# Cache attention with score products over 256 keys, turned five channel slices at a time

## The chip, the core and the metric

The kernel runs on one core of a Trainium2 chip. The metric is the device time of one execution in microseconds (us). Of the core's engines, TensorE (PE in the profile; PEld is its weight load) does the matrix products, VectorE (DVE), ScalarE (ACT) and GpSimd (POOL) the rest, and POOL also issues the gathers of this text. SyncE (SP) issues most other transfers. Each engine runs its instructions in the order in which the built program lists them, and waits on semaphores for the others.

## The reference, cut to what matters

The program is one inference step of a two-layer decoder: layer 0 mixes tokens with an mLSTM, layer 1 with multi-head latent attention, and each layer ends in a SwiGLU feed-forward part. It serves one prompt of 1024 new tokens and 8 samples with one new token each. The change lies in layer 1, in the attention of the samples over their caches:

```
# per sample: 8192 past tokens in 64 pages of 128, 8 heads
c_all  = concat(cache_latent[pages], c_new)      # (8193, 256)
kr_all = concat(cache_k_rope[pages], kr_new)     # (8193, 64)
s = (q_lat @ c_all.T + q_rope @ kr_all.T) * SCALE   # (8, 8193)
o = softmax(s) @ c_all                              # (8, 256)
```

The caches are float32. A sample's cached keys are 8192 rows of 256 latent and 64 rotary channels, 10.5 MB, and all 8 samples read 84 MB.

## The kernel before

Layer 1's attention stage runs two things side by side. The prompt's attention is cut into 32 slots (8 heads, 4 blocks of 256 queries; `prompt`, L1700): scores (L1725 to L1732), softmax (L1733 to L1749), transposes of the weights on PE (L1765), their split into a high and a low part (`split_g`, whose low part is L130 on POOL, or `split`, L117 and L118), and the product with the values (L1785). Between the slots `sample_units` (L1850) is advanced, a Python generator. It makes 16 units: each of the 8 samples has two, of 4096 cached keys. `NONE` and `DBL` say after which slots it is advanced not at all, or twice.

A unit in the kernel before is worked in two halves of 2048 keys (`u`):

- Gathers on POOL's queue: two of latent rows into `nat` (L1877, 1 MB each) and two of rotary rows into `nrp` (L1878, 256 KB each). `nat` has four buffers of [128, 16, 256] floats, two units' worth; a buffer comes free when the value products of the unit two before have read it. `nrp` has two.
- Five transposes on DVE (L1885), each of 1024 elements per partition, turn two slices of 32 channels of the half into a `tt` tile (four buffers). I call one **T**.
- Score products on PE (L1892) into `psS`, half of the PSUM tile `ss`: the stationary operand is `qbd`, 128 x 32, and the moving one 128 x 128, a block of turned keys; the four values of `j` write four groups of 32 PSUM partitions. They come in two bursts for a half, one of three `tt` tiles (24 products) and one of two (16). I call such a burst **M**. A float32 product is two records in the trace, so 48 and 32 there.

After both halves the unit's softmax runs (L1897 to L1913): row maximum on DVE, exponential on ACT, one transpose and 16 small copies into `pz`. The value products (L1921, `values()`), **V**, multiply `pz` (128 x 32) with `nat` (256 columns), 32 products or 64 records. They are recorded as `self.due` and written only at the start of the next unit, or inside the next prompt slot. The second unit of a sample is followed by a short epilogue (L1925 to L1943).

What sets the order: the code is not run in the order written. A scheduler in the tile framework places each instruction by its dependences and its own estimate of times; `high_priority(offset=SOON)` lets M and V move ahead of other work, and `issue_after(self.qk)` keeps V behind a prompt product. So a change inside a unit moves the instructions around it on every engine of the stage. Outside the stage the two programs list the same instructions in the same order.

Of the kernel before, what the change touches and what calls it, by code (L numbers as in the profile page):

```python
# [18 lines left out]
P = 128  # L19
# [72 lines left out]
class Kern:  # L92
# [15 lines left out]
    def t(self, pool, shape, tag, dt=F32, bufs=None):  # L108
        self.n += 1
        return pool.tile(shape, dt, tag=tag, name=f"{tag}{self.n}", **({"bufs": bufs} if bufs else {}))  # L110
# [1739 lines left out]
    def sample_units(self, b, first):  # L1850
        nc = self.nc
        V = nc.vector
        pr = self.pr
        t = lambda shape, tag, bufs: self.t(pr, shape, tag, bufs=bufs)
        lat = self.cache_latent.rearrange("l n (r s) c -> (l n r) (s c)", s=8)
        rop = self.cache_k_rope.rearrange("l n (r s) c -> (l n r) (s c)", s=8)
# [8 lines left out]
            self.nb = self.nb0[:, b:b + 1]  # L1865
        ss = self.mmt("ss")
        psS, psV = ss[:, 0:256], ss[:, 256:512]
        keys = []
        for u in range(2):
            nat = t([P, 16, 256], "nat", 4)  # L1870
            nrp = t([P, 16, 64], "nrp", 2)
            keys.append(nat)
            for g in range(2):
                n = b * 8 + (0 if first else 4) + u * 2 + g
                ix = bass.IndirectOffsetOnAxis(ap=self.idx[:, n:n + 1], axis=0)
                s = slice(g * 8, g * 8 + 8)
                nc.gpsimd.indirect_dma_start(out=nat[:, s].rearrange("p s c -> p (s c)"), out_offset=None, in_=lat, in_offset=ix)  # L1877
                nc.gpsimd.indirect_dma_start(out=nrp[:, s].rearrange("p s c -> p (s c)"), out_offset=None, in_=rop, in_offset=ix)  # L1878

            for cps in ((4, 0, 1), (2, 3)):  # L1880
                parts = []
                for cp in cps:
                    tt = t([P, 2, 16, 32], "tt", 4)
                    src = nat[:, :, 64 * cp:64 * cp + 64] if cp < 4 else nrp
                    V.transpose(out=tt, in_=src.rearrange("p s (c i) -> p c s i", i=32))  # L1885
                    parts.append((cp, tt))
                with self.tc.high_priority(offset=SOON):
                    for cp, tt in parts[-1:] + parts[:-1]:
                        for c in range(2):
                            cb = 2 * cp + c  # L1890
                            for j in range(4):
                                nc.tensor.matmul(psS[32 * j:32 * j + 32, u * P:u * P + P], self.qbd[:, b, cb],  # L1892
                                                 tt[:, c, 4 * j:4 * j + 4].rearrange("p s k -> p (s k)"), start=cb == 2, stop=cb == 5)
            if u == 0:
                yield
        rm = t([P, 1], "rm", 2)
        V.reduce_max(rm, psS, axis=AX.X)  # L1897
# [11 lines left out]
        pz = self.pz  # L1909
# [6 lines left out]
        def values():  # L1916
            self.due = None
            with self.tc.high_priority(offset=SOON), self.tc.issue_after(self.qk):
                for i in range(8):
                    for j in range(4):  # L1920
                        nc.tensor.matmul(psV[32 * j:32 * j + 32], pz[:, j, i], keys[i // 4][:, j * 4 + i % 4], start=i == 0, stop=i == 7)  # L1921
            V.scalar_tensor_tensor(acc, acc, al, psV, op0=ALU.mult, op1=ALU.add)
            if not first:
                m = t([P, 1], "m", 1)
                V.tensor_scalar(m, nb, -1.0, None, op0=ALU.mult)  # L1925
                nc.tensor.transpose(ss[0:1, 0:P], m, self.ident)
                mn = t([1, 8], "mn", 1)
                V.reduce_max(mn, ss[0:1, 0:P].rearrange("o (x h) -> o h x", h=8), axis=AX.X)
                mc = t([P, 256], "sS", 1)[0:1, :P].rearrange("o (x h) -> o x h", h=8)
                V.tensor_copy(mc, mn.unsqueeze(1).to_broadcast([1, 16, 8]))  # L1930
                nc.tensor.matmul(ss[:, P:P + 1], mc.rearrange("o x h -> o (x h)"), self.ones[0:1, 0:1], start=True, stop=True)
                fac = t([P, 1], "fac", 2)
                V.tensor_tensor(fac, m, ss[:, P:P + 1], op=ALU.subtract)
                nc.scalar.activation(fac, fac, AF.Exp)
                V.tensor_scalar(lrow, lrow, fac, None, op0=ALU.mult)
                nc.tensor.matmul(ss[:, 256:257], self.ct[:, C_SL:C_SL + P], lrow, start=True, stop=True)
                rl = t([P, 1], "rl", 2)
                V.reciprocal(rl, ss[:, 256:257])
                w = t([P, 8], "w0", 2)
                V.tensor_scalar(w, self.ct[:, C_SL:C_SL + 8], rl, fac, op0=ALU.mult, op1=ALU.mult)  # L1940
                for f in range(2):
                    nc.tensor.matmul(ss[:, 384 + f * 8:392 + f * 8], acc[:, f * P:(f + 1) * P], w, start=True, stop=True)
                V.tensor_copy(self.olat[:, :, :, b], ss[:, 384:400].rearrange("p (f h) -> p f h", f=2))  # L1943
# [166 lines left out]
```

## Time and profile before

| | |
|---|---|
| median of 3 runs | 2581.78 us (2577.17 to 2588.86) |
| the profiled execution | 2603.12 us, span of its instructions 2601.3 us |
| PE, PEld, DVE busy | 2510.5, 2367.6, 1864.6 us |
| ACT, POOL busy | 1328.5, 606.3 us |
| M: records, busy | 2560, 101.7 us |
| V: records, busy | 1024, 62.3 us |
| T: instructions, busy | 160, 192.4 us |
| gathers | 128 (64 `nat`, 64 `nrp`), by issue on POOL 60.8 and 61.5 us |

A row of a group reads: line, engine, operation, out<-in by the program's tile names, shape, xcount | busy us, mean ns of one | idle time of the engine just before them, and what ended most of it. Busy time is a union: products in flight at once count once. A row of the timeline reads: start in us from the span's start, length, engine, line, operation, tiles, shape, xcount; equal neighbours are merged, so a burst is one row, and its end is when its last result is out. The time to the next row's start is the better measure of what it holds PE for.

### The profile page before, as it was taken

How to read it: one execution, taken by the hardware profiler on the slowest of the kernel's cores; microseconds unless marked ns; L12 is line 12 of the kernel's file. 1: busy time of each engine (PE TensorE's matmuls, PEld its weight loads, DVE VectorE, ACT ScalarE, POOL GpSimd, SP SyncE). 2: the span in 40 equal slices, each digit the busy share in tenths (PEclk: the TensorE clock that was granted, in tenths of full speed). 3: DMA queues.
4: the chain of work that ended last, by engine and by line, in shares of the span. 5: the costliest groups of instructions: out<-in, count | busy, mean ns of one | idle time of the engine just before them, and what ended most of it. 6: DMA issues, size and time to landing. Idle time of an engine off the chain costs nothing.

```text
span 2601.3 us, 54299 instructions
## 1 busy us (share of the span) xinstructions
PE 2510.5 (97%) x21151; PEld 2367.6 (91%) x21151; DVE 1864.6 (72%) x4491; ACT 1328.5 (51%) x3282; POOL 606.3 (23%) x636
## 2 busy tenths in 40 slices
PE   8999999999999999999988889999999999999998
PEld 8999987999999999999976767767899999999998
DVE  4345678897777777666557877768498877777765
ACT  4122344465666666554354555656256656556543
POOL 1021222201111111122335545442211111111102
PEclk9999999999999999999988999999999999999999
DMA  6153554427666566654566676664535566665663
GB/s 196 41 83 95 147 138 106 157 78 149 121 129 124 115 122 128 122 163 150 192 226 247 237 259 225 210 242 147 191 106 113 119 129 127 130 127 115 122 137 113
DMA packets 332087, 382.35 MB, mean 147 GB/s; under 512 B 23433, under 2 KB 263054, under 8 KB 323510
## 3 DMA queue, kind: packets, MB, share of 16 engines
q0 software_dynamic: 60992, 186.65, 31.9%
q1 hardware_dynamic: 258838, 182.04, 23.3%
q10 hardware_dynamic: 12000, 10.20, 1.2%
q8 instruction: 166, 2.72, 0.4%
q14 instruction: 91, 0.75, 0.1%
HBM read 253.37 MB, written 125.44 MB: 146 GB/s over the span
## 4 chain that ended last, share of the span: by engine, by line
PE 69%; DVE 9%; DMA 4%; issue 4%; ACT 2%; POOL 1%; SPq 0%; another core or an unknown queue 0%; POOLq 0%; ACTq 0%; DVEq 0%
PE sc L136 12%; PE sc L134 12%; PE sc L135 12%; PE mm L136 5%; PE mm L135 5%; PE mm L134 5%; PE ss L1892 2%; PE ss L134 2%; PE ss L135 2%; PE ss L136 2%; DMA nat<-in_cache_latent_dram,idx 2%; PE ss L1921 2%; DVE tt L1885 2%; PE mm L1785 1%; DVE wl L118 1%
## 5 line engine op out<-in xcount | busy, mean ns | idle before, releaser
L1215 POOL DMA_DIRECT2D x_d<-wl x72 | 86.8, 1206 | 992.6 <-DVE wl L1214 357.1
L117 ACT ACTIVATE wh<-wr 128x512 fp32r<-128x512 f32 (+2 forms) x167 | 133.4, 799 | 199.7 <-PE mm L135 136.1
L1885 DVE STREAM_TRANSPOSE tt<-nat 128x1024 f32<-128x1024 f32 x128 | 155.4, 1228 | 28.6 <-DMA nat<-in_cache_latent_dram,idx 20.4
L1892 PE MATMUL ss<-tt,qbd 128*32 128x128 f32 x2560 | 101.7, 289 | 18.2 <-issue 8.3
L1892 PEld LDWEIGHTS ss<-tt,qbd 128*32 128x32 f32 x2560 | 76.9, 115 | 40.7 <-issue 17.7
L118 DVE TENSOR_TENSOR wl<-wr,wh 128x1024 fp32r<-128x1024 f32 (+2 forms) x80 | 92.8, 1161 | 28.2 <-ACT wh L117 27.0
L117 ACT ACTIVATE b<-u 128x256 fp32r<-128x256 f32 (+1 forms) x252 | 98.5, 414 | 20.4 <-PE ss L136 6.3
L118 DVE TENSOR_TENSOR b<-u,b 128x256 fp32r<-128x256 f32 (+1 forms) x252 | 103.1, 422 | 6.8 <-ACT b L117 5.4
L1215 POOL DMA_DIRECT2D x_d<-st x72 | 102.4, 1422 | 8.6 <-DVE dC L118 3.5
L134 PE MATMUL mm<-zh,wh 128*128 128x344 f32 x320 | 103.5, 323 | 0.0
L135 PE MATMUL mm<-zl,wh 128*128 128x344 f32 x320 | 103.4, 323 | 0.0
L136 PE MATMUL mm<-zh,wl 128*128 128x344 f32 x320 | 103.3, 323 | 0.0
L118 DVE TENSOR_TENSOR wh<-S,wh 128x512 fp32r<-128x512 f32 x108 | 74.5, 690 | 34.6 <-ACT wh L117 34.3
L117 ACT ACTIVATE wh<-S 128x512 fp32r<-128x512 f32 x108 | 67.9, 629 | 44.4 <-PE sc L136 32.1
L1742 ACT ACTIVATE wr<-sc,mx,rqt 128x512 f32<-128x512 f32 (+2 forms) x96 | 64.6, 676 | 39.5 <-DVE mx L1737 22.8
L134 PE MATMUL sc<-zh,wh 128*128 128x344 f32 x256 | 82.9, 325 | 0.2 <-DVE q L432 0.2
L1785 PE MATMUL mm<-wh,vt 128*128 128x256 f32 (+1 forms) x320 | 74.6, 298 | 8.5 <-ACT wh L117 6.3
L135 PE MATMUL sc<-zl,wh 128*128 128x344 f32 x256 | 82.1, 321 | 0.0
L136 PE MATMUL sc<-zh,wl 128*128 128x344 f32 x256 | 82.0, 320 | 0.0
L1878 POOL DMA_INDIRECT nrp<-in_cache_k_rope_dram,idx x64 | 61.5, 961 | 64.5 <-DVE tt L1885 30.2
L905 POOL TENSOR_TENSOR ss<-ss,sq 128x512 f32<-128x512 f32 (+2 forms) x36 | 51.2, 1423 | 99.4 <-ACT sq L904 99.3
L130 POOL TENSOR_TENSOR wl<-spl,wh 128x512 fp32r<-128x512 f32 x43 | 54.7, 1284 | 83.4 <-ACT spl L129 80.8
(1084 smaller groups left out, 10701.6 us busy)
## 6 DMA issues: line engine op xcount, KB each, us to landing
wr<-in_ffn_w_gate_up_dram SPq DMA_DIRECT2D x96, 512.0 KB
x_d<-st POOLq DMA_DIRECT2D x72, 520.0 KB
x_d<-wl POOLq DMA_DIRECT2D x72, 512.0 KB
dr<-in_ffn_w_down_dram SPq DMA_DIRECT2D x72, 256.0 KB
wr<-in_mlstm_w_in_dram SPq DMA_DIRECT2D x24, 512.0 KB
wr<-in_mlstm_w_out_dram SPq DMA_DIRECT2D x16, 512.0 KB
q<-qn_d SPq DMA_DIRECT2D x28, 256.0 KB
wr<-in_mla_w_o_dram SPq DMA_DIRECT2D x14, 512.0 KB
```

Of the source, the lines that this page charges most:

```text
L117: ins = nc.scalar.activation(hi, src, AF.Copy)
L118: self.low = e.tensor_tensor(lo, src, hi.bitcast(F32), op=ALU.subtract)
L130: nc.gpsimd.tensor_tensor(lo, x, hi.bitcast(F32), op=ALU.subtract)
L134: mm(ps, wh, xh, start=start, stop=False, **kw)
L135: mm(ps, wh, xl, start=False, stop=False, **kw)
L136: self.last = mm(ps, wl, xh, start=False, stop=stop, **kw)
L1215: nc.gpsimd.dma_start(self.x_d[:, 2 * dp:2 * dp + 2, 512 * i:512 * i + 2 * PW[i]], st[i], accum_op=ALU.add)
L1742: nc.scalar.activation(px[:, ks], o, AF.Exp, bias=mx[:, 0:1], scale=f, accum_out=sm[:, c:c + 1])
L1785: nc.tensor.matmul(o, x, y, start=i == 0, stop=i == len(ops) - 1)
L1878: nc.gpsimd.indirect_dma_start(out=nrp[:, s].rearrange("p s c -> p (s c)"), out_offset=None, in_=rop, in_offset=ix)
L1885: V.transpose(out=tt, in_=src.rearrange("p s (c i) -> p c s i", i=32))
L1892: nc.tensor.matmul(psS[32 * j:32 * j + 32, u * P:u * P + P], self.qbd[:, b, cb], tt[:, c, 4 * j:4 * j + 4].rearrange("p s k -> p (s k)"), ...
```

## The change

A unit is no longer worked by halves of keys, but by channels. All eight gathers of a unit are issued first, each rotary one before the latent one, into a `nat` of both halves (two buffers, the same bytes) and an `nrp` of both (one buffer, the same bytes). A T turns one slice of 32 channels of both halves. A product moves 256 columns, 128 keys of each half, so a unit has 40 of them (80 records) in place of 80 (160 records). Step 0 turns and multiplies channel slices 0, 8, 9 and then 1, 2 (8 and 9 are the rotary ones); step 1 turns 3, 4, 5 and then 6, 7. There are four bursts in a unit as before, of 12 and 8 products.

```diff
-        keys = []
+        nat = t([P, 2, 16, 256], "nat", 2)
+        nrp = t([P, 2, 16, 64], "nrp", 1)
         for u in range(2):
-            nat = t([P, 16, 256], "nat", 4)
-            nrp = t([P, 16, 64], "nrp", 2)
-            keys.append(nat)
             for g in range(2):
...
-                nc.gpsimd.indirect_dma_start(out=nat[:, s].rearrange("p s c -> p (s c)"), out_offset=None, in_=lat, in_offset=ix)
-                nc.gpsimd.indirect_dma_start(out=nrp[:, s].rearrange("p s c -> p (s c)"), out_offset=None, in_=rop, in_offset=ix)
-
-            for cps in ((4, 0, 1), (2, 3)):
+                nc.gpsimd.indirect_dma_start(out=nrp[:, u, s].rearrange("p s c -> p (s c)"), out_offset=None, in_=rop, in_offset=ix)
+                nc.gpsimd.indirect_dma_start(out=nat[:, u, s].rearrange("p s c -> p (s c)"), out_offset=None, in_=lat, in_offset=ix)
+
+        for step in range(2):
+            for cbs in ((0, 8, 9), (1, 2)) if step == 0 else ((3, 4, 5), (6, 7)):
                 parts = []
-                for cp in cps:
+                for cb in cbs:
                     tt = t([P, 2, 16, 32], "tt", 4)
-                    src = nat[:, :, 64 * cp:64 * cp + 64] if cp < 4 else nrp
-                    V.transpose(out=tt, in_=src.rearrange("p s (c i) -> p c s i", i=32))
-                    parts.append((cp, tt))
+                    src = nat[:, :, :, 32 * cb:32 * cb + 32] if cb < 8 else nrp[:, :, :, 32 * cb - 256:32 * cb - 224]
+                    V.transpose(out=tt.rearrange("p u s k -> p (u s) k"), in_=src.rearrange("p u s c -> p (u s) c"))
+                    parts.append((cb, tt))
                 with self.tc.high_priority(offset=SOON):
-                    for cp, tt in parts[-1:] + parts[:-1]:
-                        for c in range(2):
-                            cb = 2 * cp + c
-                            for j in range(4):
-                                nc.tensor.matmul(psS[32 * j:32 * j + 32, u * P:u * P + P], self.qbd[:, b, cb],
-                                                 tt[:, c, 4 * j:4 * j + 4].rearrange("p s k -> p (s k)"), start=cb == 2, stop=cb == 5)
-            if u == 0:
+                    for cb, tt in parts[-1:] + parts[:-1]:
+                        for j in range(4):
+                            nc.tensor.matmul(psS[32 * j:32 * j + 32], self.qbd[:, b, cb],
+                                             tt[:, :, 4 * j:4 * j + 4].rearrange("p u s k -> p u (s k)"), start=cb == 9, stop=cb == 6)
+            if step == 0:
                 yield
...
-                        nc.tensor.matmul(psV[32 * j:32 * j + 32], pz[:, j, i], keys[i // 4][:, j * 4 + i % 4], start=i == 0, stop=i == 7)
+                        nc.tensor.matmul(psV[32 * j:32 * j + 32], pz[:, j, i], nat[:, i // 4, j * 4 + i % 4], start=i == 0, stop=i == 7)
```

In the program after, M is L1889, V is L1918, T is L1884, and the gathers are L1875 (`nrp`) and L1876 (`nat`). The scheduler's order moves with it. Two places show how; the number behind a tile's name tells the allocations apart.

PE, around the value products of the thirteenth unit (`ss_20857`). Before, the first bursts of the fourteenth unit (`ss_21205`) stand ahead of them, and those of its second half behind:

```order
L1892 MATMUL ss_21205<-tt_21244,qbd_16070 32x128 x8
L1892 MATMUL ss_21205<-tt_21242,qbd_16070 32x128 x8
...
L1732 MATMUL sc_21102<-mk_15334 128x128
L1921 MATMUL ss_20857<-nat_20858,pz_15338 32x256 x16
L1921 MATMUL ss_20857<-nat_20994,pz_15338 32x256 x16
L1892 MATMUL ss_21205<-tt_21379,qbd_16070 32x128 x8
L1892 MATMUL ss_21205<-tt_21375,qbd_16070 32x128 x8
L1892 MATMUL ss_21205<-tt_21377,qbd_16070 32x128 x8
```

After, the same two units are `ss_20353` and `ss_20659`:

```order
L1732 MATMUL sc_20556<-mk_15334 128x128
L1918 MATMUL ss_20353<-nat_20354,pz_15338 32x256 x32
L1889 MATMUL ss_20659<-tt_20674,qbd_16070 32x256 x4
L1889 MATMUL ss_20659<-tt_20670,qbd_16070 32x256 x4
L1889 MATMUL ss_20659<-tt_20672,qbd_16070 32x256 x4
L1785 MATMUL mm_20464<-wh_20454,vt_20013 128x256
```

The first burst of a unit has moved from ahead of the value products of the unit before it to behind them, and each row of products is half as many of twice the width.

POOL, the gathers of the tenth unit and the splits of the prompt (L130) near them. Before, the rotary gathers of the tenth (`nrp_19615`, `nrp_19778`) and eleventh unit are issued early, and the tenth unit's latent ones (`nat_19614`) behind several splits:

```order
L1878 DMA nrp_19615<-in_cache_k_rope_dram,idx_14527 128x512 x2
L1878 DMA nrp_19778<-in_cache_k_rope_dram,idx_14527 128x512 x2
L130 TENSOR_TENSOR kt_18510<-spl_18640,kt_18510 128x512
L130 TENSOR_TENSOR kt_18510<-spl_18651,kt_18510 128x512
L1878 DMA nrp_20043<-in_cache_k_rope_dram,idx_14527 128x512 x2
L130 TENSOR_TENSOR wl_18832<-spl_18838,wh_18831 128x512
L130 TENSOR_TENSOR wl_18832<-spl_18847,wh_18831 128x512
L130 TENSOR_TENSOR vt_18883<-spl_18897,vt_18883 128x512
L130 TENSOR_TENSOR wl_18996<-spl_19002,wh_18995 128x512
L1877 DMA nat_19614<-in_cache_latent_dram,idx_14527 128x2048 x2
```

After, the ninth unit's eight gathers (`nrp_18931`, `nat_18930`) stand together ahead of the splits around them:

```order
L130 TENSOR_TENSOR wl_18319<-spl_18325,wh_18318 128x512
L1875 DMA nrp_18931<-in_cache_k_rope_dram,idx_14527 128x512 x4
L1876 DMA nat_18930<-in_cache_latent_dram,idx_14527 128x2048 x4
L130 TENSOR_TENSOR kt_18242<-spl_18372,kt_18242 128x512
L130 TENSOR_TENSOR kt_18242<-spl_18383,kt_18242 128x512
L130 TENSOR_TENSOR wl_18538<-spl_18544,wh_18537 128x512
L130 TENSOR_TENSOR wl_18538<-spl_18553,wh_18537 128x512
```

A unit's gathers have moved closer to each other, and splits of the prompt now stand behind four latent gathers in a row.

## The prediction

> **What bounds the kernel now.** I read the page first, then the stage in which the units run, by windows, groups, waits, the chain, and the timeline of single bursts.
>
> ```profile
> span 2601.3 us, 54299 instructions
> PE 2510.5 (97%) x21151; PEld 2367.6 (91%) x21151; DVE 1864.6 (72%) x4491; ACT 1328.5 (51%) x3282; POOL 606.3 (23%) x636
> L1892 PE MATMUL ss<-tt,qbd x2560: 269/273/423, 1355.6 to 1779.0; 128*32 128x128 f32 x197
> 1350.00:1790.00 440.00, 394.31 (x5021) 308.38 (x5020) 329.90 (x715) 238.36 (x630) 210.08 (x206) 0.96 0.67 231
> by line: PE ss L1892 14.5%; DMA nat<-in_cache_latent_dram,idx 11.6%; issue 10.0%; PE ss L1921 9.8%; DVE tt L1885 9.2%; PE mm L1785 7.7%; PE mm L1765 2.7%; POOL wl L130 2.5%; DVE pz L1913 2.3%; POOL nrp L1878 2.0%; PE sc L1725 1.9%; PE sc L1
> ```
>
> The third line bounds the stage: M starts at 1355.6 and 1779.0, so I take 1350 to 1790, 440 us of 2601. In this window (PE, PEld, DVE, ACT, POOL busy; PE clock; DMA share; GB/s) PE is busy 394 of 440 us, DVE 330, the DMA engines 0.67. Over the page PE has 97%, here 90%. The last line is the chain in this window: a quarter of it runs through M and the latent gathers' flight, a further fifth through T and V. So PE is nearly full but does not bound the stage alone; the units' own circle (V frees a buffer, gather, T, M, softmax, V) is often what ends last. Nothing outside this stage is touched, so the forecast is a sum over it.
>
> The groups of this window and the waits in it (us in total, times, longest):
>
> ```profile
> L1885 DVE STREAM_TRANSPOSE tt<-nat 128x1024 f32<-128x1024 f32 x128 | 155.4, 1228 | 28.6 <-DMA nat<-in_cache_latent_dram,idx 20.4 <-PE ss L1892 4.2 <-remote 3.5
> L1892 PE MATMUL ss<-tt,qbd 128*32 128x128 f32 x2560 | 101.7, 289 | 18.2 <-issue 8.3 <-DVE tt L1885 7.3 <-DVE sm L1745 1.7
> L1892 PEld LDWEIGHTS ss<-tt,qbd 128*32 128x32 f32 x2560 | 76.9, 115 | 40.7 <-issue 17.7 <-DVE tt L1885 15.0 <-DVE sm L1745 3.5
> L1921 PE MATMUL ss<-nat,pz 128*32 128x256 f32 x1024 | 62.3, 381 | 1.3 <-ACT pz L1913 0.9 <-issue 0.4
> PE ss L1892 <- DVE tt L1885: 7.3, 9, 3.0
> POOL nat L1877 <- PE ss L1921: 14.2, 7, 5.6
> POOL nrp L1878 <- DVE tt L1885: 30.2, 9, 8.2
> POOL wl L130 <- ACT spl L129: 80.8, 18, 17.0
> PE mm L1785 <- ACT wh L117: 5.8, 7, 2.1
> PE mm L1785 <- POOL wl L130: 0.5, 2, 0.3
> ```
>
> The reader is to see that M waits 18.2 us in all (PE idle ahead of it), V 1.3, that T waits 20.4 us for latent gathers, that those wait for V (14.2) and the rotary ones for T (30.2), and that PE hardly ever waits for POOL's split (0.5).
>
> **The change part by part. The products.** 1280 products of 128 columns (2560 records) become 640 of 256 (1280 records). What is a product worth? The group's mean of 289 ns says nothing, since four column groups overlap. The timeline of PE shows bursts without a wait in them:
>
> ```profile
> 1427.56 0.40 PE L1728 MATMUL sc<-kk,qrr 128*128 128x512 f32 x1
> 1427.79 0.39 PE L1730 MATMUL sc<-kl,qrr 128*128 128x512 f32 x1
> ...
> 1593.18 0.28 PE L134 MATMUL mm<-swh,ckh 128*128 128x256 f32 x1
> 1593.30 0.27 PE L135 MATMUL mm<-swl,ckh 128*128 128x256 f32 x1
> 1593.71 1.52 PE L1892 MATMUL ss<-tt,qbd 128*32 128x128 f32 x48
> 1595.16 0.39 PE L136 MATMUL mm<-swh,ckl 128*128 128x256 f32 x1
> ...
> 1596.06 1.08 PE L1892 MATMUL ss<-tt,qbd 128*32 128x128 f32 x32
> 1597.07 0.39 PE L136 MATMUL mm<-swh,ckl 128*128 128x256 f32 x1
> ...
> 1598.84 3.75 PE L1921 MATMUL ss<-nat,pz 128*32 128x256 f32 x64
> 1602.33 1.68 PE L1892 MATMUL ss<-tt,qbd 128*32 128x128 f32 x38
> ```
>
> From start to the next start, 48 records hold PE for 1.45 us and 32 for 1.01. The 16 between them, four groups of four, cost 0.44: 0.110 us for a group of 128 columns, and 1.01 - 8 x 0.110 = 0.13 us is left for the burst, whatever its length. V has the very shape that M gets (32 stationary columns, 256 moving, float32): 64 records, 16 groups, 3.49 us, so 0.218 for a group of 256. Two narrow groups, 0.220, become one wide, 0.218. There are 320 such pairs, so the change saves 0.6 us of PE in 2600. The 0.13 of a burst stays, as there are still four bursts in a unit. If I divide each burst by its records instead, 0.0302 for M (1.45 / 48) and 0.0545 for V, the unit would go from 4.92 to 80 x 0.0545 = 4.36 us, 9.0 us in all; that counts the burst's own 0.13 as the records', and V followed directly by M doesn't pay it. So 0.6, with 0 and 9.0 as ends.
>
> The Trainium skill's page "TensorEngine Tiling (Array Packing)", section Instruction Overhead, gives each matmul about 60 cycles beside its columns, which at the 2.4 GHz of its page "TensorE: Matmul & The Clock Gate" would be, as an estimate, 1280 x 25 ns = 32 us saved. That second page of the Trainium skill, section Back-to-back issue gap, has N / 2.4 + 2.5 ns from one to the next instead, which gives an estimate of 320 x 2.5 ns = 0.8 us. The trace agrees with the second and not with the first: 0.110 and 0.218 us for twice 128 and twice 256 columns.
>
> Two edits go with it. 1280 weight loads fall away; they lie beside the products (76.9 us in PEld, and the 0.110 of a group already holds whatever of them shows): 0. Entering and leaving the narrow form costs PE the 0.13; counted over PE's order the changes between 32 and 128 stationary columns go from 142 to 138, since V and M follow each other more often: -0.3, between 0 and -0.5.
>
> **The transposes.** 160 of 1024 elements before and after, with the same runs of 32 floats: 0 by the row (1228 ns). Nothing covers more than that: at 30 ns more or less each, DVE would have 5 us more or less in 440, of which it is busy 330.
>
> **The gathers and the waits.** This is where the time can move. The same 128 gathers, 0.95 us of POOL each, carry the same bytes. But the first T of a unit (slice 0) now needs all four latent gathers, where it needed two. The price of a pair, from V to T, in the rows of PE, POOL and DVE:
>
> ```profile
> 1456.05 4.01 PE L1921 MATMUL ss<-nat,pz 128*32 128x256 f32 x64
> 1459.69 0.96 POOL L1877 DMA_INDIRECT nat<-in_cache_latent_dram,idx  x1 [0.16 <-issue]
> 1460.96 0.94 POOL L1877 DMA_INDIRECT nat<-in_cache_latent_dram,idx  x1 [0.30 <-issue]
> 1469.03 1.25 DVE L1885 STREAM_TRANSPOSE tt<-nat 128x1024 f32<-128x1024 f32 x1 [3.22 <-DMA nat<-in_cache_latent_dram,idx]
> q0 software_dynamic: 14185, 81.56, 52.4%
> ```
>
> From the first issue to T it is 9.3 us for 2.1 MB. The last row (packets, MB, share of 16 engines in the 440 us) gives the gathers' full rate, 81.56 MB / (0.524 x 440 us) = 354 GB/s: 5.9 us of data, 3.4 around it. Four latent gathers, 4.2 MB, then take 11.8 + 3.4 = 15.2 us, and 18.2 if the 1.05 MB of the rotary ones falls among them. So the first T comes 6 to 9 us later after V than before.
>
> Against it stands more cover. In PE's order I summed the rows between the end of a unit's V and the first M of the unit two later (the one that gets its buffer), each at its pace: 0.110 and 0.218 for groups as above, 0.12 for a 256-wide product (1593.18 to 1593.30), 0.23 for a 512-wide (1427.56 to 1427.79). Over the 14 units it is 9.7 us before (5.3 to 13.2), 18.5 after (15.4 to 22.2): the first M has gone behind the V of the unit ahead of it, as the two pieces of PE's order show. The whole stage sums to 308 us at that pace and takes 440, a stretch of 1.43, so the cover is about 14 us before and 26 after. Needed: before 9.3 + two T, 11.8; after 15.2 to 18.2 + three T, 18.9 to 21.9. The margin of a unit rises from 2 us to between 4 and 7. So I expect fewer waits of T on gathers, and of M on T: a third of M's 18.2, -6, between -18.2 (all of it) and +28 (the slower rival).
>
> What pays for it is the way from a unit's last M to its V, in which the softmax runs: 14.9 us at the same pace before, 7.5 after, and 3.2 to 4.5 in the first five units, 4.6 to 6.4 stretched. The chain's rows have such a way nearly bare:
>
> ```profile
> 1396.44 0.81 PE ss L1892 x18
> ...
> 1402.59 0.40 issue
> 1402.99 4.02 PE ss L1921 x60
> ```
>
> 5.7 us from M's end (1397.25) to V, of which V waited the last 0.40. So V will wait up to a microsecond in the first five units, +3 (0 to 6). And the first unit starts later, since nothing is turned until its fourth latent gather, which now stands behind two splits into `kt`. Its rows in POOL and DVE now:
>
> ```profile
> 1351.70 0.94 POOL L1877 DMA_INDIRECT nat<-in_cache_latent_dram,idx  x1 [0.30 <-issue]
> 1352.65 2.54 POOL L130 TENSOR_TENSOR kt<-spl,kt 128x512 fp32r<-128x512 f32 x2
> 1352.00 1.25 DVE L1885 STREAM_TRANSPOSE tt<-nrp 128x1024 f32<-128x1024 f32 x1 [2.36 <-DMA nrp<-in_cache_k_rope_dram,idx]
> ```
>
> With the splits first, the gather goes out near 1354 and lands some 8 us later (1460.96 to 1469.03 above), 10 us after the 1352.0 at which T begins now. But all ten T of that unit can then follow without a break, and the scheduler has put the first M behind 5 us more of the prompt's products: +1 (0 to 7).
>
> **The sum:** -0.6 - 0.3 - 6 + 3 + 1 = -3 us. The profiled execution took 2603.12 us (1.8 more than its span), 21 above the median of the runs; on it that is 2600, on the median, 2581.8, it is 2579. A measurement of this kernel tells a change of about 0.5%, 13 us, from none.
>
> **The rivals.** *Waits go too (faster).* If the margin is as large as I work out, M may stop waiting at all: -18.2 for M, less the 3 for V and 1 for the start, gives 2567, more if the prompt's products wait less as well. For it speaks the margin; against it that a third of M's idle time is put down to DVE's order and not to gathers, as the transposes of a unit still take 10 x 1.23 us of an engine that has 330 of 440 us of work.
>
> *Cost by the instruction (faster).* If a wide group cost what a narrow one does, M would lose 320 x 0.110 = 35 us: 2547. V's 0.218 speaks against it; only a difference between V's weights or addresses and M's could save it. The first rule of the Trainium skill above ("TensorEngine Tiling (Array Packing)", Instruction Overhead) is on this side.
>
> *The gathers bind (slower).* Each unit's gathers are now one block on POOL, four in a row behind one V, and the prompt's splits (L130) behind them, as the pieces of POOL's order show; a rotary gather of the next unit can't go until T has turned this unit's, which is behind the latent gathers now. If the block's last gather lands over 22 us after V instead of 15 to 18, the cover of 26 us is used up by it and three T. Each microsecond beyond holds M, and with it PE, in 14 units: at 2 us, +28, 2610. The up to 5.6 us that a latent gather waited for V and up to 8.2 of a rotary one on T speak for it, the 0.5 us that PE waited for splits against. The clock is a part of it: over 1400 to 1500 PE was granted 0.95 of it.
>
> ```profile
> 1400.00:1500.00 100.00, 90.42 (x1206) 71.34 (x1205) 78.01 (x168) 50.92 (x140) 52.40 (x52) 0.95 0.69 236
> ```
>
> The Trainium skill's page "TensorE: Matmul & The Clock Gate", section What's actually happening, halves the clock after an idle window of about 3.4 us; one such window in each of the 14 units would by that, as an estimate, cost 14 x 1.7 = 24 us more. The longest wait of M for T in the rows above is 3.0 us, so no run here shows that step yet.
>
> **How the numbers follow.** No change that can be told 0.46 (2579); waits go too 0.28; cost by the instruction 0.03; the gathers bind 0.23. So faster 0.31, same 0.46, slower 0.23. The range reaches past the first faster case, 8 us below its 2567, and into the slower one, 2602, which leaves out about 0.08 below and 0.12 above. The likeliest case alone has 2569 to 2594.
>
> **What would show it.** M: 1280 records, bursts of 24 and 16 that hold PE for 1.44 and 1.00 us (0.13 + 6 or 4 x 0.218); busy of the group near 95 us, not 60 to 80. T: 160 of 1.23 us. The wait of T on latent gathers below 20.4 us, V's idle time up from 1.3 to some 4, M's down from 18.2 to about 12. The stage from 1350 on within 10 us of 440. I am wrong if a burst of 24 is under 1.2 us (cost by the instruction), or if T's wait on gathers or POOL's on V grows and PE's idle time ahead of M or L1785 with it.

## The result: 25 us slower, and the profile after

The changed kernel takes 2607.07 us (median of 5, 2601.22 to 2610.6), the kernel before beside it 2581.78: 1.0095 times as long, interval 1.0076 to 1.0114. Forecast was 2579 with a range to 2602, so the forecast is wrong; the case that came is *the gathers bind*.

The page and the window of the stage after, in the order of the rows shown before (span; engines; M's group in the window; the window's busy times, clock and DMA; the chain):

```profile
span 2605.3 us, 51742 instructions
PE 2500.6 (96%) x19871; PEld 2333.0 (90%) x19871; DVE 1867.0 (72%) x4491; ACT 1328.2 (51%) x3282; POOL 604.7 (23%) x636
L1889 PE MATMUL ss<-tt,qbd 128*32 128x256 f32 x1280 | 89.6, 410 | 27.2 <-DVE tt L1884 24.6 <-DVE sm L1745 2.3
1350.00:1790.00 440.00, 381.94 (x3658) 271.73 (x3656) 327.32 (x704) 233.11 (x616) 205.35 (x202) 0.94 0.66 226
by line: DMA nat<-in_cache_latent_dram,idx 14.3%; PE ss L1889 12.4%; DVE tt L1884 9.2%; issue 8.3%; PE mm L1785 5.9%; PE ss L1918 4.7%; DMA acc<-cn_d 2.8%; PE mm L1765 2.7%; ACT wr L1742 2.5%; POOL wl L130 2.1%; POOL nrp L1875 2.0%; ACT spl
```

M waits 27.2 us in place of 18.2 (9.2 in a second profile of the kernel before, below), nearly all of it for T, and the latent gathers' share of the chain has risen from 11.6 to 14.3%. The groups and waits (us in total, times, longest) of the same window:

```profile
L1884 DVE STREAM_TRANSPOSE tt<-nat 128x1024 f32<-128x1024 f32 x128 | 152.4, 1220 | 34.9 <-DMA nat<-in_cache_latent_dram,idx 26.7 <-PE ss L1889 3.9 <-DMA acc<-cn_d 3.5
L1918 PE MATMUL ss<-nat,pz 128*32 128x256 f32 x960 | 60.6, 399 | 3.5 <-ACT pz L1910 3.5
POOL nrp L1875 <- DVE tt L1884: 42.3, 9, 9.2
POOL nat L1876 <- PE ss L1918: 29.4, 7, 7.6
POOL wl L130 <- ACT spl L129: 34.8, 12, 17.1
```

POOL is held longer ahead of gathers: by T 42.3 us (30.2 before), by V 29.4 (14.2 before). The wait of its splits into `wl` for ACT has fallen from 65.9 to 34.8 us in this window (the 80.8 shown ahead of the change is for a window that begins at 1320).

The first profile of the kernel before took 21 us more than the median of its runs; a second one of the same kernel (e0_before below) has a span of 2589.2 at a clock of 0.982, the clock of the profile after. From the first gather to the end of the last V these two compare as follows (second profile of before, then after):

```profile
1321.20:1778.90 457.70, 406.92 (x5097) 321.20 (x5096) 335.01 (x739) 253.85 (x668) 216.29 (x212) 0.93 0.67 229
1321.60:1794.60 473.00, 407.92 (x3829) 290.88 (x3829) 336.90 (x739) 254.81 (x669) 216.30 (x212) 0.93 0.66 224
```

The stage is 15.3 us longer (473.0 against 457.7), the spans differ by 16.1, PE is busy as long, and its idle time (length less busy) went from 50.8 to 65.1: **14.3 us more idle time of PE**, at the same clock. T, M and V in this second profile of before (window 1340 to 1800):

```profile
L1885 DVE STREAM_TRANSPOSE tt<-nat 128x1024 f32<-128x1024 f32 x128 | 155.3, 1227 | 35.3 <-DMA nat<-in_cache_latent_dram,idx 28.2 <-PE ss L1892 6.9
L1892 PE MATMUL ss<-tt,qbd 128*32 128x128 f32 x2560 | 92.1, 289 | 9.2 <-DVE tt L1885 7.3 <-DVE sm L1745 0.9 <-DVE olat L1943 0.2
L1921 PE MATMUL ss<-nat,pz 128*32 128x256 f32 x1024 | 63.9, 395 | 4.2 <-ACT pz L1913 4.2
```

M's idle time is 9.2 us here and 27.2 after. T's wait for the latent gathers is no longer after (26.7 against 28.2): what changed is that PE now waits for T.

For the rest the clock is the candidate: over 116 runs of eight kernels, 0.001 of the mean clock of a run goes with 1.9 us within one kernel. The five runs of after had 0.9818 on average, 25 later runs of before 0.9862, which would be 8 us. So some 15 us are idle time, and some 8 go with a lower granted clock; that second figure is an estimate, as no run changes the clock alone.

One unit's gathers in POOL's rows, after. V two units ahead (start, length) ended at 1569.6:

```profile
1565.65 3.91 PE L1918 MATMUL ss<-nat,pz 128*32 128x256 f32 x64 [0.26 <-ACT pz L1910]
1569.94 0.96 POOL L1875 DMA_INDIRECT nrp<-in_cache_k_rope_dram,idx  x1 [4.20 <-DVE tt L1884]
1571.21 0.94 POOL L1876 DMA_INDIRECT nat<-in_cache_latent_dram,idx  x1 [0.30 <-issue]
...
1576.19 0.94 POOL L1876 DMA_INDIRECT nat<-in_cache_latent_dram,idx  x1 [0.30 <-issue]
1579.52 1.27 POOL L130 TENSOR_TENSOR vt<-spl,vt 128x512 fp32r<-128x512 f32 x1 [2.39 <-ACT spl L129]
1581.22 1.29 POOL L130 TENSOR_TENSOR wl<-spl,wh 128x512 fp32r<-128x512 f32 x1 [0.43 <-POOL vt L130]
1582.65 0.97 POOL L1875 DMA_INDIRECT nrp<-in_cache_k_rope_dram,idx  x1
1583.92 0.93 POOL L1876 DMA_INDIRECT nat<-in_cache_latent_dram,idx  x1 [0.31 <-issue]
1592.37 1.25 DVE L1884 STREAM_TRANSPOSE tt<-nat 128x1024 f32<-128x1024 f32 x1 [3.07 <-DMA nat<-in_cache_latent_dram,idx]
1596.73 1.50 PE L1889 MATMUL ss<-tt,qbd 128*32 128x256 f32 x24 [2.48 <-DVE tt L1884]
1596.86 1.01 POOL L1875 DMA_INDIRECT nrp<-in_cache_k_rope_dram,idx  x1 [7.22 <-DVE tt L1884]
```

The reader sees that the last of four latent gathers goes out 14.4 us behind V: rotary gathers stand between the latent ones on POOL, the first of them held 4.20 us by T (all but 0.4 of it before V's end), and two splits stand ahead of the last pair, one of which waits for ACT. T starts 8.5 us later, M waits 2.48 for it, and the next unit's rotary gather has been held 7.22 us by this unit's T.

This is the rule and not the exception. Of the third to sixteenth unit the ninth, whose order on POOL was shown ahead of the prediction, is the only one with nothing but gathers between its first and its last latent gather, and there they go out within 3.7 us. In the others one to five splits or writes of `acc` stand between, and the mean of all is 13.4 us (9.5 in the second profile of before). Worked out from POOL's rows, the mean of 14.5 us from V to the last latent issue holds 5.3 us of the gathers' own issue, 4.3 of splits and their waits for ACT, 1.6 of the writes of `acc` and their wait for PE, and 1.0 of waits for T; the rest is small.

### The profile page after: what moved, and what is told of

Same layout as the page of the kernel before. It is cut to its first block, busy times and chain, and to the rows that moved or that the text cites. A ratio compares the mean times of both kernels' runs of the same rounds, so it can differ in the third digit from the quotient of the medians.

```text
span 2605.3 us, 51742 instructions
## 1 busy us (share of the span) xinstructions
PE 2500.6 (96%) x19871; PEld 2333.0 (90%) x19871; DVE 1867.0 (72%) x4491; ACT 1328.2 (51%) x3282; POOL 604.7 (23%) x636
## 4 chain that ended last, share of the span: by engine, by line
PE 68%; DVE 10%; DMA 5%; ACT 3%; issue 3%; POOL 1%; SPq 0%; ACTq 0%; POOLq 0%; DVEq 0%
PE sc L134 12%; PE sc L136 12%; PE sc L135 12%; PE mm L136 5%; PE mm L134 5%; PE mm L135 5%; DMA nat<-in_cache_latent_dram,idx 2%; PE ss L1889 2%; PE ss L134 2%; PE ss L136 2%; PE ss L135 2%; DVE tt L1884 2%; DVE wl L118 1%; PE mm L1785 1%; PE ss L1918 1%
## 5 line engine op out<-in xcount | busy, mean ns | idle before, releaser
L1884 DVE STREAM_TRANSPOSE tt<-nat 128x1024 f32<-128x1024 f32 x128 | 152.4, 1220 | 34.9 <-DMA nat<-in_cache_latent_dram,idx 26.7
L1889 PE MATMUL ss<-tt,qbd 128*32 128x256 f32 x1280 | 89.6, 410 | 27.2 <-DVE tt L1884 24.6
L118 DVE TENSOR_TENSOR wl<-wr,wh 128x1024 fp32r<-128x1024 f32 (+2 forms) x80 | 92.8, 1161 | 27.1 <-ACT wh L117 26.7
L117 ACT ACTIVATE b<-u 128x256 fp32r<-128x256 f32 (+1 forms) x252 | 98.5, 414 | 20.4 <-PE ss L136 6.3
L1889 PEld LDWEIGHTS ss<-tt,qbd 128*32 128x32 f32 x1280 | 38.3, 115 | 60.3 <-DVE tt L1884 28.9
L1785 PE MATMUL mm<-wh,vt 128*128 128x256 f32 (+1 forms) x320 | 77.2, 305 | 6.6 <-ACT wh L117 3.2
L1785 PEld LDWEIGHTS mm<-wh,vt 128*128 128x128 f32 x320 | 57.3, 202 | 22.9 <-issue 8.6
L1875 POOL DMA_INDIRECT nrp<-in_cache_k_rope_dram,idx x64 | 61.3, 958 | 67.5 <-DVE tt L1884 42.3
```

Of the source, the lines that this page charges most:

```text
L117: ins = nc.scalar.activation(hi, src, AF.Copy)
L118: self.low = e.tensor_tensor(lo, src, hi.bitcast(F32), op=ALU.subtract)
L1785: nc.tensor.matmul(o, x, y, start=i == 0, stop=i == len(ops) - 1)
L1875: nc.gpsimd.indirect_dma_start(out=nrp[:, u, s].rearrange("p s c -> p (s c)"), out_offset=None, in_=rop, in_offset=ix)
L1884: V.transpose(out=tt.rearrange("p u s k -> p (u s) k"), in_=src.rearrange("p u s c -> p (u s) c"))
L1889: nc.tensor.matmul(psS[32 * j:32 * j + 32], self.qbd[:, b, cb], tt[:, :, 4 * j:4 * j + 4].rearrange("p u s k -> p u (s k)"), start=cb == 9 ...
```

## The experiments

The columns are: ratio to the kernel before, run beside each (its medians were 2580 to 2597 us, so ratios are compared and not times); then, as means over the third to sixteenth unit, worked from the rows of gathers, T, M and V: the time from the end of the V that frees the buffer to the issue of the unit's last latent gather, and to its first M; then PE's idle time from the first gather to the last V.

| kernel | ratio [95%] | last latent issue | first M | PE idle |
|---|---|---|---|---|
| before, once more | 1.0002 [0.9982, 1.0022] | 8.9 | 15.2 | 51 |
| after | 1.0095 [1.0076, 1.0114] | 14.5 | 28.2 | 65 |
| e1_narrow | 1.0085 [1.0051, 1.0119] | 15.7 | 29.3 | 73 |
| e2_early | 1.0030 [1.0016, 1.0044] | 11.9 | 16.9 | 58 |
| e3_rotary | 1.0008 [0.9993, 1.0024] | 10.7 | 22.0 | 54 |
| e4_latfirst | 1.0029 [1.0012, 1.0046] | 10.6 | 26.3 | 60 |
| e6_rotfirst | 1.0022 [1.0004, 1.0041] | 12.8 | 27.1 | 58 |
| e5_both | 1.0015 [0.9999, 1.0030] | 10.8 | 21.5 | 55 |
| e8_delay | 1.0095 [1.0069, 1.0121] | 16.7 | 27.1 | 64 |
| e9_bdelay | 1.0099 [1.0073, 1.0124] | 16.2 | 19.0 | 68 |
| e10_brot | 0.9987 [0.9970, 1.0004] | 9.2 | 13.7 | 52 |
| e11_bfree | 1.0138 [1.0114, 1.0161] | 10.8 | 16.6 | 74 |
| e12_free | 1.0064 [1.0039, 1.0089] | 11.8 | 23.3 | 69 |
| e13_nolat | 0.9997 [0.9986, 1.0007] | 11.5 | 10.7 | 59 |
| e14_bnolat | 1.0041 [1.0022, 1.0060] | 8.5 | 7.6 | 65 |
| e15_nudge | 1.0075 [1.0058, 1.0092] | 14.3 | 28.1 | 69 |
| e16_rnudge | 0.9989 [0.9978, 1.0001] | 10.2 | 22.5 | 60 |
| e17_bnudge | 1.0039 [1.0025, 1.0054] | 10.4 | 15.2 | 59 |

The edits are shown shortened.

**The width, the split units, and the slices first.** The kernel before once more:

> The kernel before once more, for a second profile beside the timed runs (the first profiled execution took 21 us longer than the median). If the 21 us were the profile's, its span is near 2600 us again; if it was that execution's own, the span is near 2580 and the stage from 1350 on is shorter than the 440 us of the first profile.

After, with each product cut in two of 128 columns:

```diff
-for j in range(4):
-    matmul(psS[32j:32j+32], qbd[b, cb], tt[:, :, 4j:4j+4])
+for u in range(2):
+    for j in range(4):
+        matmul(psS[32j:32j+32, u*P:u*P+P], qbd[b, cb], tt[:, u, 4j:4j+4])
```

> The changed kernel with each product cut into two of 128 columns (one for each half of the unit); gathers, transposes and steps as in the change. Width theory (a product costs by its columns): M's bursts hold PE for 1.45 and 1.01 us in place of 1.44 and 1.00, time within 1 us of the changed kernel but for the order, so 2595 to 2620. If the width were worth 9 us or more, 2616 and up. If the loss came from the wide form (two runs of keys in one operand), this one is back near 2582.

Before, with a unit's eight gathers in one block (rotary ones first, buffers for a whole unit), but T and M still by halves:

> The kernel before with one part of the change: all eight gathers of a unit first, rotary ahead of latent, in buffers of the whole unit (two latent, one rotary); transposes and products by halves of the keys, 128 columns wide, as before. Theory A (the first transposes of a unit wait for all four latent gathers): not here, since the first half needs two, so near 2582. Theory B (the single rotary buffer and the block of gathers hold POOL's queue): the loss is here too, 2600 to 2612. Theory C (any edit makes the scheduler draw another order, and that alone moves the time): anywhere from 2570 to 2615.

After, with the rotary slices turned ahead of the latent one:

```diff
-for cbs in ((0, 8, 9), (1, 2)) if step == 0 else ((3, 4, 5), (6, 7)):
+for cbs in ((8, 9, 0), (1, 2)) if step == 0 else ((3, 4, 5), (6, 7)):
```

> The changed kernel with step 0 turning slices 8, 9, 0 in place of 0, 8, 9, so that the two rotary slices, whose gathers are issued first, are turned while the latent ones still fly, and the rotary buffer comes free 2.4 us and a latent flight sooner. Theory A: a unit's first burst needs one transpose in place of three after the last latent gather, 2.4 us in up to 14 units, so up to 34 us faster than the changed kernel, 2575 to 2595. Theory B: POOL's rotary gathers wait much less for transposes than 42 us. If neither is the cause: 2600 to 2615.

Narrow products in the changed kernel give 2607.86 us (ratio 1.0085), so the width carries none of the loss that could be told. One block of gathers with T by halves costs 0.3% (2591.65 us, between the ranges of theories A and B). Turning slices 8 and 9 first, an exchange of three numbers (the start flag of the products moves with it), takes the loss away (2585.53 beside 2585.05). The rows of M narrow, and of M and POOL's wait with 8 and 9 first; M's row after stands above:

```profile
L1890 PE MATMUL ss<-tt,qbd 128*32 128x128 f32 x2560 | 92.6, 294 | 38.6 <-DVE tt L1884 34.4 <-DVE sm L1745 3.4
```
```profile
L1889 PE MATMUL ss<-tt,qbd 128*32 128x256 f32 x1280 | 87.5, 398 | 22.1 <-DVE tt L1884 20.7 <-DVE sm L1745 0.8
POOL nrp L1875 <- DVE tt L1884: 15.1, 4, 8.7
```

With 8 and 9 first POOL is held by T 15.1 us in place of 42.3, the last latent gather goes out 10.7 us behind V in place of 14.5, and only one T in place of three stands between its landing and M.

**The order of the gathers.** After, with the block's loops exchanged: four latent gathers, then four rotary ones; the reverse; and the reverse together with slices 8 and 9 first.

```diff
-for u in range(2):
-    for g in range(2):
-        gather nrp[u, g]; gather nat[u, g]
+for rot in (0, 1):          # (1, 0) in the other two
+    for u in range(2):
+        for g in range(2):
+            gather (nrp if rot else nat)[u, g]
```

> The kernel after, with the four latent gathers of a unit issued ahead of its four rotary ones; the transposes keep their order (slices 0, 8, 9, then 1, 2). Theory B (POOL's queue: the latent gathers stand behind rotary ones, which wait for the transposes of slices 8 and 9 of the unit before): from the end of the value products to the issue of the last latent gather it takes 5 to 6 us in place of 14.5, the first score product comes 18 to 20 us after them in place of 28.2, and the time falls to 2580 to 2592. Theory A (the first transpose waits for four gathers' data and three transposes lie ahead of the products): the chain is the same length, 2600 to 2612. Theory C (any edit of this block draws another order of the scheduler, which by itself moves the time by some 20 us): no link between the time and the issue of the last latent gather.

> The kernel after, with the four rotary gathers of a unit issued ahead of its four latent ones; an edit of the same size as that of latents first, and the transposes keep their order (0, 8, 9, then 1, 2). Theory B: all four latent gathers now stand behind all four rotary ones, whose buffer comes free only when slices 8 and 9 of the unit before are turned, which stand behind slice 0 of it: no better than after, 2605 to 2625, with the last latent gather 14 us or more behind the value products. Theory A: unchanged, 2600 to 2612. Theory C: anywhere between 2575 and 2625, on no side of latents first that could be told ahead.

> Slices 8 and 9 turned ahead of slice 0, as in the run that recovered the loss, and besides the four rotary gathers issued ahead of the four latent ones. Theory B: the rotary buffer comes free before the latent slices are waited for, so the rotary gathers are out early and the four latent ones go in a row behind the value products: last latent issue 4 to 7 us behind them in place of 10.7, the first score product some 17 us, idle time of the score products 10 to 16 us in place of 22.1, time 2570 to 2582, faster than both kernels. Theory A: the four latent gathers are still waited for as one, no change against the run with 8 and 9 first, 2583 to 2590. Theory C: anywhere between 2575 and 2625.

Latents first comes to the time that the theory of POOL's queue (B) said, 2591.48 us, but not by its way: the last issue was to be at 5 to 6 us and the first M at 18 to 20, and they are at 10.6 and 26.3. Rotary first was to stay at 2605 to 2625 by B and gives 2589.66, with the last issue at 12.8. Theory A had 2600 to 2612 for both and fails in both. So "latent gathers stuck behind rotary ones" is too narrow, and so is the wait for four gathers by itself. A block of one kind in either order is some 0.6% better than the two kinds in turn, which is little more than the 0.4% by which the last runs below show that an order alone can move the time. e5_both gains nothing over e3_rotary, where B had 2570 to 2582 and a last issue at 4 to 7 us in place of 10.8.

**Putting the delay back.** POOL writes zeros over the place of a unit's third and fourth latent gather just ahead of them, in e3_rotary and in the kernel before; and e10_brot exchanges each latent gather with its rotary one in the kernel before.

```diff
+if u == 1:
+    nc.gpsimd.memset(nat[:, u, s], 0.0)
 indirect_dma_start(out=nat[:, u, s], ...)
```

> The run with slices 8 and 9 turned first, which lost nothing, with POOL writing zeros over the places of a unit's third and fourth latent gather just ahead of them: the output is the same, and the last latent gather goes out later by two writes of an estimated 2 us each. Circle theory (value products free the buffer, gathers, transposes, score products, softmax, value products of two units later; the time is lost once this circle has no slack): from the end of the value products to the last latent issue 14 to 16 us in place of 10.7, to the end of the unit's score products 38 to 40 in place of 34.1, as in the changed kernel (40.2): the loss comes back, 2597 to 2612, with PE idle 62 to 70 us in the stage in place of 54. Theory C (the order that the scheduler happens to draw): the delay is covered, 2580 to 2592.

> The kernel before with the same two writes of zeros ahead of the latent gathers of a unit's second half. Circle theory: its score products end 28.2 us behind the value products that free the buffer and leave 22.7 us to the unit's own value products, so 4 us more are covered: 2580 to 2592. Theory C: anywhere between 2575 and 2612.

> The kernel before with each rotary gather issued ahead of the latent one beside it, as the changed kernel has it, and nothing else. Circle theory: the circle has slack in the kernel before, so no change that can be told, 2578 to 2590. Theory B (rotary gathers ahead of latent ones on POOL are what costs): the latent gathers stand behind rotary ones, which wait some 30 us in all for transposes; the last latent issue 2 to 4 us later than 8.9, 2588 to 2605. Theory C: anywhere between 2575 and 2612.

```profile
L1877 POOL MEMSET nat<- 128x2048 f32 x32 | 57.4, 1816 | 0.0
```

In e8_delay the loss is back, as the theory of the circle had it: PE idle 64 us, 2605.52 us, with the last issue at 16.7 us, a little beyond its 14 to 16. But e9_bdelay, which was to be covered, loses as much (2606.5), so either the kernel before has no cover either, or the writes cost in another way. e10_brot shows no change that can be told (0.9987, the interval holds 1), as the circle theory said; B had it 2588 to 2605 and it takes 2578.98.

**POOL's time by itself.** Thirty writes of 32 columns a unit, which nobody reads, in the kernel before and in e3_rotary:

```diff
+z = t([P, 32], "zz", 1)
+for _ in range(30):
+    nc.gpsimd.memset(z, 0.0)
```

> The kernel before, with POOL writing zeros into a small place of its own that nobody reads: thirty writes of 32 columns a unit, an estimated 3.7 us a unit, the time of the two writes in the run of before that delayed the gathers (3.6 us a unit, 57.7 in all), but tied to no gather. Theory of the late gather (what costs is the issue of the last latent gather behind the value products: 8.9 us in the kernel before, 16.2 in the delayed one): the writes fall into POOL's waits, the last latent issue stays below 12 us, 2576 to 2594. Theory POOL (the writes cost through POOL's time itself, or through what they hold up on other engines): 2597 to 2612, as with the delayed gathers.

> The run with slices 8 and 9 turned first, with the same thirty small writes of POOL a unit, tied to no gather. Theory of the late gather: last latent issue below 13 us behind the value products (10.7 without the writes, 16.7 with the gathers delayed), 2580 to 2595. Theory POOL: 2597 to 2612, as with the delayed gathers (2605.5).

```profile
L1883 POOL MEMSET zz<- 128x32 f32 x480 | 61.1, 127 | 22.6
```

The theory of the late gather fails here: the last issue stays at 10.8 and 11.8 us, as it said, and yet the ratios are 1.0138 and 1.0064. In e12_free M idles no more than in e3_rotary (19.5 us against 22.1); the prompt's products do instead (L1785, 256 columns, 16.2 us against 1.0). In e11_bfree a part does run through the gathers: T waits 41.0 us for latent ones (28.2 in the second profile of before) and M 20.4 for T (7.3). So time on POOL can cost without a later gather, or the order drawn with the writes does, and the two runs with delayed gathers prove less than they seemed to: how much of their loss is the late gather isn't settled.

**Taking the wait away.** That is free of POOL's time: the latent T read a tile that is always there, so the scores leave the gathered latent channels out.

```diff
-src = nat[:, :, :, 32 * cb:32 * cb + 32] if cb < 8 else nrp[...]
+src = (32 slices of qbd) if cb < 8 else nrp[...]
```

> The kernel after, with the eight latent transposes of a unit reading a tile that is always there in place of the gathered latent slices; all gathers stay, the value products still read them, the rotary transposes still wait for their gathers (so scores and output are not the reference's). If the loss of 25 us passes through the wait of the transposes for the latent gathers, it goes away: the idle time of the score products falls from 27 to 5 to 15 us, and the time comes within 13 us of that of the same edit in the kernel before, 2560 to 2590. If it passes through POOL's time, the wider transposes in a row, or the form of the products, the time stays 15 us or more above the same edit in the kernel before.

> The kernel before, with the same edit: the latent transposes read a tile that is always there. It has little of this wait to lose (9 to 18 us of idle time ahead of the score products): 2565 to 2585. What matters is its distance to the same edit in the kernel after: under 13 us if the transposes' wait for the latent gathers carries the loss, 15 us or more below it if another thing does.

The changed kernel is level with the kernel before (0.9997), and the kernel before becomes slower by the same edit (1.0041). So 2596.2 stands beside 2606.0, both above their forecasts, on a chip where the kernel before takes 2596.7: without T's wait for latent gathers the changed form is not slower. M's idle time was to fall to 5 to 15 us and did not; the rows of M in the changed form and in the form before:

```profile
L1889 PE MATMUL ss<-tt,qbd 128*32 128x256 f32 x1280 | 88.0, 401 | 31.2 <-DVE tt L1884 10.6 <-issue 9.8 <-DVE sm L1745 6.1
```
```profile
L1892 PE MATMUL ss<-tt,qbd 128*32 128x128 f32 x2560 | 100.0, 291 | 34.5 <-DVE tt L1885 17.0 <-issue 8.6 <-DVE acc L1922 5.2
```

Here M is early in the order that the scheduler draws and waits for DVE's turn and for the softmax of the prompt. M's idle time alone is thus no measure of the loss, and an order drawn anew can cost 0.4% by itself.

**Other orders.** Next to no work, but another order: three small writes of POOL a unit in after, one small write of DVE in e3_rotary, six of POOL in the kernel before.

> The kernel after with three small writes of POOL a unit (0.127 us each by the earlier run, 6 us of POOL in all) that nobody reads: almost no work, but the scheduler draws another order from it (about a thousand rows of PE's order differ). Structure theory (all four latent gathers are waited for, and the first transpose is a latent one): the loss stays, ratio to before 1.005 to 1.014. Theory C (the loss belongs to one drawn order): ratio 0.996 to 1.004 as likely as any.

> The run with slices 8 and 9 turned first, with one small write of DVE a unit that nobody reads, from which the scheduler draws another order. Structure theory: still no loss, ratio to before 0.998 to 1.004. Theory C: anywhere from 0.996 to 1.012.

> The kernel before with six small writes of POOL a unit (0.127 us each, 12 us of POOL in all) that nobody reads, from which the scheduler draws another order. Structure theory: no loss, ratio to before 0.998 to 1.004. Theory C: anywhere from 0.996 to 1.012.

The changed form stays slow in another order (1.0075), its repaired form stays level (0.9989), and the kernel before moves by 0.4% (1.0039, of which the writes' 12.5 us of POOL may be a part). So the loss is not that of one unlucky order, as far as one more order of each tells; which order is drawn shifts a kernel by up to some 0.4%. As far as these runs show, it needs both slice 0 turned first and the two kinds of gathers in turn: without either it was 0.3% at most.

## Why the prediction was wrong, point by point

- **Products, -0.6: right.** Bursts of 24 and 16 records hold PE for 1.43 and 1.00 us from start to next start (1.44 and 1.00 were forecast), and e1_narrow has 1.45 and 1.01 for the narrow form. That rules out *cost by the instruction*, and with it the rule of the Trainium skill's page "TensorEngine Tiling (Array Packing)", section Instruction Overhead, for products like these.

```profile
1419.17 1.50 PE L1889 MATMUL ss<-tt,qbd 128*32 128x256 f32 x24
1420.60 0.50 PE L136 MATMUL mm<-ckh,swl 128*128 128x512 f32 x1
...
1421.73 1.07 PE L1889 MATMUL ss<-tt,qbd 128*32 128x256 f32 x16
1422.73 0.50 PE L134 MATMUL mm<-ckh,swh 128*128 128x512 f32 x1
```

- **Changes between the forms, -0.3: not shown.** It is too small for any run here to tell.
- **Transposes, 0: right** (1220 ns against 1228).
- **V's wait, +3: not shown.** It is 3.5 us in the window after against 1.3 in the first profile of before, but 4.2 in the second, so two executions of one kernel differ by as much.
- **The first unit, +1: too low perhaps.** Its first M came 40.8 us after the first gather (1321.6 to 1362.4) in place of 28.3 before (1327.3 to 1355.6), and waited 4.91 us, which lies in the range given (0 to 7); no run tells what of that shows at the end.
- **The gathers and waits, -6: the step that failed.** It took four latent gathers to be issued in a row behind V, so that the first T would be ready 15.2 to 18.2 us behind it and the first M at 18.9 to 21.9, inside a cover of 26. The last issue alone came 14.5 us behind V, T 8.4 later, 22.9, and M at 28.2. The cover was sized well: without the wait right ahead of it, the first M would have come 26.9 us behind V (15.0 in the second profile of before, where 14 was forecast). It was the need that grew into it: 22.9 and three T of 1.23 are 26.6. Because the units differ (T at 16.5 to 31.4 us), PE waited ahead of the first M in 8 of the 14 units, 18.1 us in all (2.9 before). The order on POOL shown for "four in a row" was that of the ninth unit, the one unit in which it holds. In the others splits and writes of `acc` stand between the gathers, and where a rotary gather is held until V has ended, it and those after it are still to be issued behind V, between the latent ones. The 42.3 us of waits for T are not the price itself, as only 1.0 us a unit of them lies behind V. e3_rotary lets the rotary gathers go earlier and leaves one T behind the last landing, and takes the loss away, as do e5_both and e16_rnudge in two other orders; e13_nolat takes the whole wait away and does the same; e15_nudge shows that it is not one unlucky order.
- **The rival *the gathers bind*** had set the point at 22 us from V to the last landing, where cover and three T meet, and T, which stands for the landing here, came at 22.9. Its place and its point were right; its chance of 0.23 was too low, and *waits go too* had the wrong sign. Its rule (each microsecond beyond holds M in 14 units) gives 0.9 x 14 = 13 us, and PE's idle time rose by 14.3; that they are so near is partly luck, since the rule takes all units as equal, and 6 of the 14 did not wait.
- **The clock was in no term of the sum.** By the estimate above it gave some 8 us more. Why the five runs of after were granted less stays open: e12_free and e15_nudge have as much idle time at other clocks (0.980 and 0.984).
- **Not settled:** which share of the 15 us is POOL held at gathers and which is the first T behind the last landing. e3_rotary mends both at once; e4_latfirst mends the first alone (10.6 us to the last issue) and wins back most of it, e6_rotfirst mends neither by much (12.8 us, first M at 27.1) and does as well, which no theory here explains.

## What to carry to other kernels

Before a wait is made wider (one operation that needs all of four transfers where it needed two), walk the queue that issues the last of them, entry by entry, in every unit and not in one, and add what stands between the release and the last entry; here the one unit shown was the only one of fourteen whose four transfers went out in a row. If a buffer's release hangs on work that itself waits for a later transfer in the same queue, do the releasing work first: here three numbers in a list were worth 22 us. Where a scheduler orders the work, redraw its order once or twice with next to no work added before a difference of half a per cent is put down to a cause.

## What the runs showed of the chip

- **Small writes of POOL are dear.** 480 writes of 128 x 32, 0.127 us each, 61 us in all on an engine that was busy 216 of 458 us, made the kernel before 1.4% slower (2628.3 beside 2593.2), though nobody reads them. DVE's transposes took as long as ever beside them (1224 ns against 1227); which part is POOL's time and which the new order isn't shown.
- **A wait can cost twice.** After an idle time of 3.56 us PE's next burst of 24 products held it 2.72 us (1462.19 to 1464.91) in place of the 1.43 above, at half the pace and a granted clock of 0.50 (the last row below); the burst of 16 behind it had its full pace again:

```profile
1462.19 2.79 PE L1889 MATMUL ss<-tt,qbd 128*32 128x256 f32 x24 [3.56 <-DVE tt L1884]
1464.91 0.47 PE L134 MATMUL mm<-swh,ckh 128*128 128x256 f32 x1
...
1465.90 1.07 PE L1889 MATMUL ss<-tt,qbd 128*32 128x256 f32 x16
1462.19:1464.91 2.72, 2.71 (x24) 0.99 (x25) 2.65 (x3) 0.00 (x0) 2.32 (x3) 0.50 0.30 74
```

The Trainium skill's page "TensorE: Matmul & The Clock Gate", section What's actually happening, has the clock halved after an idle window of about 3.4 us and released after as long a busy one; the trace agrees in this row. It doesn't need so long an idle time, though. The prediction said that no run had shown that step, but the first profile of the kernel before has it, where PE's longest idle time in the 5 us ahead was 1.00 us:

```profile
1369.70:1373.10 3.40, 1.20 (x11) 0.67 (x11) 0.00 (x0) 0.46 (x1) 2.37 (x3) 1.00 1.00 355
1373.20:1379.90 6.70, 5.73 (x37) 5.33 (x38) 3.60 (x6) 2.03 (x7) 0.95 (x1) 0.50 0.77 318
```

PE was busy 1.20 of 3.40 us in several short pieces at the full clock, and then had half of it for the next 6.70. So many short waits can cost clock as one long one does, and a longest wait of 3.0 us was no ground to leave the step out.
